# A planner's rule that holds VectorE and ScalarE for urgent operations, an earlier landing time, and 18 idle products instead of 22

## The chip, the cores and the metric

The kernel runs on 1 core of one Trainium2 chip. The metric is the device time of one execution in microseconds (us). The median of three runs of the kernel before is 561.59 us, the lowest 561.55, the highest 562.51.

The names of the engines: TensorE is PE in the rows (PEld is its weight load), VectorE is DVE, ScalarE is ACT, GpSimd is POOL and SyncE is SP, which issues most transfers.

## The reference

Two layers of a decoder trunk over 256 positions of width 1024. Each layer makes RMSNorm of x, one wide input projection (5452 + 3072 columns), and from its parts three token mixers: a gated DeltaNet (short convolution, chunked delta rule with a triangular solve, 4 heads), a pooling mixer, and sparse attention in which an indexer picks 64 keys per query. Their outputs are gated, projected, merged and projected again.

```python
def hybrid_layer(x, ...):
    h = rms_norm(x, norm_g)
    proj = jnp.einsum('btd,de->bte', h, w_in)
    (qa, ka, va, za, ba, aa, ub, zb, qc, kc, vc, zc, iq, ik, iw, gates) = split_columns(proj)
    ya = deltanet_branch(qa, ka, va, za, ba, aa, conv_w, a_log, dt_bias, dn_onorm)
    yb = pooling_branch(ub, zb, pool_w, pool_scale)
    yc = sparse_attention_branch(qc, kc, vc, zc, iq, ik, iw, q_norm, k_norm, ...)
    branches = jnp.stack([ya, yb, yc], axis=2)
    projected = jnp.einsum('btnc,ncd->btnd', branches, w_branch)
    gate = jax.nn.sigmoid(gates.reshape(b, t, N_BRANCH, D_MODEL) + gate_b)
    return x + jnp.einsum('btd,de->bte', jnp.sum(gate * projected, axis=2), w_out)
```

In DeltaNet the decay is the exponential of differences of a cumulative sum g, and the solve is of a unit lower triangular matrix per chunk of 64. In the attention, scores outside the chosen keys are put to minus infinity before the softmax.

## The kernel before

Activations and weights are float32; TensorE multiplies them as three products of a shorter type: a weight tile comes by DMA into `raw` (5 buffers of 128 x 1024), a CAST makes its high part `wh` (6 buffers, ScalarE, or VectorE where the planner chooses it), VectorE subtracts and makes the low part `wl` (5 buffers). In the same way the normed input is `hh` and `hl`. TensorE then does wh with hh, wh with hl, and wl with hh, into one of four PSUM banks `pj`; other products and transposes go to four banks `mx`.

The order of the work is not written by hand. The code lists every operation with what it reads and writes (`Plan.add`), and `Plan.lay_out` sorts the list onto the five engines with a model of each engine's time (`cost`), of the transfers' landing times, and of the delay from one engine to another (`LAG`, and `MARGIN` of 400 ns for TensorE). On each engine the operation that is ready and has the least rank comes next; the rank is the order in the program for TensorE, and elsewhere the latest start `late`, which `deadlines` works out backwards from the end of the last pass. Six passes (`PASSES`) are made and the shortest kept. Each engine then runs its instructions in that order and waits for others by semaphores. A buffer or PSUM bank goes to the next user when its last reader is done in the plan.

`pick` chooses the next operation of one engine at the time that the engine is free. `soon` holds operations that become ready later, `now` those that are ready. `EARLY` is a time in ns that is added to a transfer's expected landing if it is issued before `CALM` (10000 ns in the plan), `DELAY` the same for later ones. The `NWARM` products at the start multiply a zeroed `wh` tile by itself and their result is not used.

Names that come up below: `gh` and `gl` are the two parts of the log decay of the heads, `sgr` a constant matrix of ones that sums them up, and the `wl` tiles written from `cs` and `gh` are the decay's factors (they take two of the `wl` buffers); `score` and `top` are the scores and the eight highest values of one round of the top-k; `big` holds the attention's logits, `sm4` their sums and `ri` their reciprocals, `nb` the negative maximum; `uc` are the diagonal 32 x 32 blocks of the triangular matrices, `xi` and `xb` belong to the recurrence that inverts them (31 steps on VectorE), `cv` is the scale of the transposed v, `u` are working tiles; `rs` is the norm's factor.

Of the kernel before, what the change touches and what calls it, by code (L numbers as in the profile page):

```python
# [42 lines left out]
LATE, X1, CRIT, BACK = 200, 138, ((-600, 0), (-600, -500)), 300  # L43

KOUT = 4
NWARM = 22

SWITCH = 103.0

# [1 line left out]

MARGIN = 400.0

EARLY, DELAY, CALM = 900.0, 900.0, 10000.0

SLACK = 300.0

LATER = 21000.0

# [207 lines left out]
class Plan:  # L267
# [168 lines left out]
    def lay_out(self):  # L436
# [12 lines left out]
        soon = {e: [] for e in engines}  # L449
        now = {e: [] for e in engines}  # L450
# [26 lines left out]
        def uses(o, e):  # L477
            return o.other[4] if o.other and e == o.other[0] else o.port

        def held(o, e):  # L480
            return o.other[2] if o.other and e == o.other[0] else o.cost

        def fill(o):
            return o.args[0].shape[0] * o.args[1].shape[0] / 16384.0

        def clear(o, e, t):


            if e in shared and uses(o, e):
                t = max(t, shared["POOL" if e == "DVE" else "DVE"])  # L490
            if e != "PE":
                for z in o.tiles:
                    if z.tag.psum and z.reader != e:
                        t = max(t, z.until)
            return t

        def live(q):
            return self.ops[q[-2]].start is None and self.ops[q[-2]].turn == q[-1]

        def pick(e):  # L500

            while soon[e] and not live(soon[e][0]):
                heapq.heappop(soon[e])
            while now[e] and not live(now[e][0]):
                heapq.heappop(now[e])
            t = free[e]
            while soon[e] and soon[e][0][0] <= t:
                q = heapq.heappop(soon[e])
                if live(q):
                    heapq.heappush(now[e], q[1:])  # L510
            if not now[e]:
                while soon[e] and not live(soon[e][0]):
                    heapq.heappop(soon[e])
                if not soon[e]:
                    return None
                q = soon[e][0][1:]
                return clear(self.ops[q[1]], e, soon[e][0][0]), e, q
            if e == "PE" and not small and t < whole + REST and fill(self.ops[now[e][0][1]]) < 0.6:
                for q in heapq.nsmallest(40, now[e]):
                    if live(q) and fill(self.ops[q[1]]) > 0.9:  # L520
                        return t, e, q
            first = now[e][0]
            at = clear(self.ops[first[1]], e, t)
            if at > t:
                for q in heapq.nsmallest(12, now[e]):
                    o = self.ops[q[1]]
                    if live(q) and clear(o, e, t) <= t and held(o, e) <= at - t + SLACK:
                        return t, e, q
            return at, e, first

        for o in self.ops:
# [3 lines left out]
        while len(order) < len(self.ops):  # L535
            best = None
            for e in engines:
                c = pick(e)
                if c and (best is None or c[:2] < best[:2]):
                    best = c  # L540
# [4 lines left out]
            at, e, q = best  # L545
            o = self.ops[q[1]]
# [85 lines left out]
def trunk(ctx: ExitStack, tc: tile.TileContext, x, xt, gain, w_in, gate_b, pool_w, w_branch, w_out, cst0, cst1, cst2, cst3,  # L632
# [44 lines left out]
    def bank(tag):  # L677
        return plan.tile(tags[tag], [128, 512])
# [66 lines left out]
    wp = bank("mx")  # L745
    for i in range(NWARM):
        PE.matmul(wp[:, :256], warm[:, :128], warm, start=True, stop=True)
# [758 lines left out]
```

## Time and profile before

| | |
|---|---|
| median of 3 runs | 561.59 us (561.55 to 562.51) |
| profiled execution | 561.43 us, span 559.50 us |
| TensorE busy | 553.1 us (99%), 3434 instructions |
| TensorE weight load busy | 487.0 us (87%) |
| VectorE busy | 499.1 us (89%), 1111 instructions |
| ScalarE busy | 325.7 us (58%), 658 instructions |
| GpSimd busy | 22.0 us (4%) |
| DMA | 99.79 MB, mean 178 GB/s |

Busy is the sum of an engine's durations. Matmuls are pipelined and their ends are modelled, so the busy time of TensorE overlaps with the next product's; the starts are the better measure. On a timeline, a row is a run of like instructions; its first number is the start of the first one, and the number in front of the engine's name is the time that they take. What stands in square brackets is the idle time in front of the row and who ended it.

### The profile page before, as it was taken

What the parts mean: (1) busy time and instruction counts of PE and PEld (TensorE: products, weight loads), DVE (VectorE), ACT (ScalarE), POOL (GpSimd) and SP (SyncE); (2) the same over time, 40 slices, a digit from 0 to 9 for tenths busy, and PEclk for the clock granted to TensorE, in tenths of its full rate; (3) what the DMA queues carried; (4) which work ended last, traced back from release to release, by engine and by line L of the source; (5) the groups of instructions that cost most, each with busy time, mean ns of one, the idle gap of its engine ahead of it and who ended that gap; (6) DMA issues with size and microseconds to landing.
All of it is one profiled execution on the core that took longest, in us unless ns stands there. A gap on an engine that the chain in (4) does not pass through costs nothing.

```text
span 559.5 us, 9552 instructions
## 1 busy us (share of the span) xinstructions
PE 553.1 (99%) x3434; PEld 487.0 (87%) x3434; DVE 499.1 (89%) x1111; ACT 325.7 (58%) x658; POOL 22.0 (4%) x31
## 2 busy tenths in 40 slices
PE   9999999999999999999999999999999999999997
PEld 8978999999888887888879789999998888788886
DVE  6999999999999999687689999799999999967672
ACT  8795786668543526463466675866584444455530
POOL 0200000000000000000010010000000000000000
PEclk9999999999999999999999999999999999999999
DMA  8845484383866656334447346346356667445402
GB/s 321 304 153 202 156 274 149 107 274 83 279 206 205 208 190 223 136 131 151 148 140 229 115 153 219 114 149 214 124 196 214 209 188 230 120 152 201 156 32 76
DMA packets 29855, 99.79 MB, mean 178 GB/s; under 512 B 3312, under 2 KB 4080, under 8 KB 29808
## 3 DMA queue, kind: packets, MB, share of 16 engines
q1 hardware_dynamic: 29232, 98.22, 53.4%
q0 software_dynamic: 288, 0.64, 0.4%
q8 instruction: 27, 0.44, 0.3%
q10 hardware_dynamic: 288, 0.33, 0.2%
q14 instruction: 20, 0.16, 0.1%
HBM read 98.12 MB, written 1.05 MB: 177 GB/s over the span
## 4 chain that ended last, share of the span: by engine, by line
PE 86%; DVE 9%; ACT 3%; issue 1%; POOL 0%; DVEq 0%; POOLq 0%
PE pj L627 69%; PE mx L627 17%; DVE wl L627 3%; DVE u L627 2%; DVE score L627 2%; ACT wh L627 1%; ACT u L627 1%; DVE top L627 1%; DVE hl L627 1%; ACT wl L627 1%; ACT big L627 0%; DVE big L627 0%; POOL r4k L627 0%; ACT uc L627 0%; ACT kiT L627 0%
## 5 line engine op out<-in xcount | busy, mean ns | idle before, releaser
L627 ACT CAST wh<-raw 128x1024 fp32r<-128x1024 f32 (+2 forms) x169 | 174.8, 1040 | 136.1 <-PE pj L627 104.5
L627 DVE TENSOR_TENSOR wl<-raw,wh 128x1024 fp32r<-128x1024 f32 (+2 forms) x176 | 209.1, 1201 | 14.4 <-PE pj L627 4.9
L627 PE MATMUL pj<-wh,hh 128*128 128x512 f32 (+1 forms) x352 | 103.0, 389 | 0.0
L627 PE MATMUL pj<-wh,hl 128*128 128x512 f32 (+1 forms) x352 | 101.2, 387 | 1.1 <-DVE hl L627 1.1
L627 PE MATMUL pj<-wl,hh 128*128 128x512 f32 (+1 forms) x352 | 101.4, 387 | 0.0
L627 PEld LDWEIGHTS pj<-wh,hl 128*128 128x128 f32 x352 | 65.2, 188 | 13.8 <-DVE hl L627 1.5
L627 PEld LDWEIGHTS pj<-wh,hh 128*128 128x128 f32 x352 | 64.6, 188 | 12.6 <-ACT hh L627 0.4
L627 PEld LDWEIGHTS pj<-wl,hh 128*128 128x128 f32 x352 | 65.0, 188 | 12.1
L627 PE MATMUL pj<-hh,wh 128*128 128x256 f32 x384 | 56.3, 285 | 0.0
L627 PE MATMUL pj<-hh,wl 128*128 128x256 f32 x384 | 55.3, 284 | 0.0
L627 PE MATMUL pj<-hl,wh 128*128 128x256 f32 x384 | 55.2, 284 | 0.0
L627 PE MATMUL pj<-wh,y 128*128 128x512 f32 (+1 forms) x208 | 51.5, 383 | 0.0
L627 PEld LDWEIGHTS pj<-hh,wh 128*128 128x128 f32 x384 | 50.4, 191 | 0.3
L627 PEld LDWEIGHTS pj<-hh,wl 128*128 128x128 f32 x384 | 50.1, 192 | 0.1
L627 PEld LDWEIGHTS pj<-hl,wh 128*128 128x128 f32 x384 | 50.0, 192 | 0.0
L627 PEld LDWEIGHTS pj<-wh,y 128*128 128x128 f32 x208 | 38.5, 188 | 7.5
L627 PE MATMUL mx<-wh,y 128*128 128x512 f32 (+1 forms) x128 | 38.4, 380 | 0.0
L627 PEld LDWEIGHTS mx<-u,u 128*128 128x128 f32 (+2 forms) x336 | 28.7, 164 | 3.0 <-issue 1.8
L627 PE MATMUL mx<-u,u 128*128 128x128 f32 (+2 forms) x336 | 30.4, 250 | 0.0
L627 DVE SCALAR_TENSOR_TENSOR u<-pj,cs,u 128x255 f32<-128x255 f32 (+2 forms) x72 | 29.1, 472 | 0.5 <-ACT u L627 0.5
L627 PE MATMUL pj<-wl,y 128*128 128x512 f32 (+1 forms) x104 | 28.5, 382 | 0.0
L627 PEld LDWEIGHTS mx<-wh,y 128*128 128x128 f32 x128 | 23.3, 188 | 4.4 <-DVE y L627 0.2
(203 smaller groups left out, 679.9 us busy)
## 6 DMA issues: line engine op xcount, KB each, us to landing
raw<-in_w_in_dram SPq DMA_DIRECT2D x124, 512.0 KB, 4.3
raw<-in_w_branch_dram SPq DMA_DIRECT2D x24, 512.0 KB, 4.4
raw<-in_w_out_dram SPq DMA_DIRECT2D x16, 512.0 KB, 3.5
tg<-in_gate_b_dram SPq DMA_DIRECT2D x12, 256.0 KB, 4.8
raw<-in_w_in_dram SPq DMA_DIRECT2D x4, 498.0 KB, 6.2
raw<-in_xt_dram SPq DMA_DIRECT2D x4, 256.0 KB, 4.3
raw<-in_xt_dram SPq DMA_DIRECT2D x2, 512.0 KB, 6.3
x_sb<-in_x_dram SPq DMA_DIRECT2D x2, 512.0 KB, 3.6
```

Of the source, the lines that this page charges most:

```text
L627: getattr(self.real[o.eng], o.call)(*[put(a) for a in o.args], **{k: put(v) for k, v in o.kw.items()})
```

## The change

Three numbers change (18 idle products, `EARLY` of 300, and a new `HASTE` of 0), and `pick` gets a rule for VectorE and ScalarE. The rule looks at the operation `o` that would be taken next and at the time `stop` at which it would end. If one of the four operations that become ready first, `z`, is ready before `stop` and its `late` is before `stop`, `o` is not taken. In its place comes another ready operation that ends before `z` is ready, or else `z` itself, for which the engine stands still until it is ready. An exception is an `o` that would itself be late if `z` went first.

```diff
-NWARM = 22
+NWARM = 18
...
-EARLY, DELAY, CALM = 900.0, 900.0, 10000.0
+EARLY, DELAY, CALM = 300.0, 900.0, 10000.0
...
+HASTE = 0.0
...
+            if e in ("DVE", "ACT"):
+                o = self.ops[first[1]]
+                stop = at + held(o, e)
+                for q in heapq.nsmallest(4, soon[e]):
+                    z = self.ops[q[2]]
+                    if live(q) and z.late is not None and q[0] < stop and z.late < stop - HASTE:
+
+                        if o.late is None or o.late < q[0] + held(z, e):
+                            break
+                        for p in heapq.nsmallest(12, now[e]):
+                            s = self.ops[p[1]]
+                            if live(p) and clear(s, e, t) + held(s, e) <= q[0] + HASTE:
+                                return clear(s, e, t), e, p
+                        return clear(z, e, q[0]), e, q[1:]
             return at, e, first
```

The orders that come of it differ in many places. TensorE has 3210 products instead of 3214 (the four idle ones). VectorE makes ten of the 128 x 1024 CASTs of `wh` instead of six, ScalarE four fewer.

VectorE at the boundary of the layers, before (numbers behind a name are buffers, `mx3_122` is a bank):

```order
L627 TENSOR_SCALAR big3_114<-big3_114,rs0_200 128x512
L627 TENSOR_TENSOR wl4_78<-raw3_66,wh2_70 128x1024
L627 TENSOR_TENSOR wl3_77<-raw4_67,wh1_69 128x1024
L627 TENSOR_TENSOR wl0_74<-raw0_63,wh4_72 128x1024
L627 TENSOR_TENSOR hl0_80<-mx1_120,hh0_79 128x4x128
L627 TENSOR_TENSOR x_sb0_123<-x_sb0_123,mx0_119 128x512
L627 TENSOR_TENSOR hl0_80<-mx3_122,hh0_79 128x4x128
```

and now:

```order
L643 TENSOR_SCALAR big3_114<-big3_114,rs0_200 128x512
L643 TENSOR_TENSOR wl3_77<-raw3_66,wh2_70 128x1024
L643 TENSOR_TENSOR wl4_78<-raw4_67,wh1_69 128x1024
L643 TENSOR_TENSOR hl0_80<-mx1_120,hh0_79 128x4x128
L643 TENSOR_TENSOR x_sb0_123<-x_sb0_123,mx0_119 128x512
L643 TENSOR_TENSOR hl0_80<-mx2_121,hh0_79 128x4x128
```

The third `wl` has moved from in front of both `hl` to behind them.

ScalarE at the decay of layer 0, before:

```order
L627 ACTIVATE wl2_76<-cs0_124,gl0_170 128x128 x4
L627 ACTIVATE eg0_171<-mx1_120 128x16
L627 ACTIVATE wl3_77<-cs0_124,gh0_169 128x128 x4
L627 ACTIVATE u4_100<-mx0_119 128x512
L627 ACTIVATE big3_114,sm40_176<-big3_114,nb0_174,r4q0_156 128x128 x4
L627 ACTIVATE wl3_77<-cs0_124,gl0_170 128x128 x2
L627 ACTIVATE big3_114<-big3_114,ri0_178 128x128
L627 ACTIVATE wl3_77<-cs0_124,gl0_170 128x128 x2
L627 ACTIVATE big3_114<-big3_114,ri0_178 128x128 x3
```

and now:

```order
L643 ACTIVATE wl2_76<-cs0_124,gl0_170 128x128 x4
L643 ACTIVATE eg0_171<-mx2_121 128x16
L643 ACTIVATE wl3_77<-cs0_124,gh0_169 128x128 x4
L643 ACTIVATE wl3_77<-cs0_124,gl0_170 128x128 x4
L643 ACTIVATE u10_106<-mx3_122 128x512
L643 ACTIVATE u11_107<-mx2_121 128x512
L643 CAST wh5_73<-raw0_63 128x1024
L643 ACTIVATE f0_94<-pj0_115 128x512
L643 CAST wh0_68<-raw1_64 128x1024
L643 ACTIVATE big3_114,sm40_176<-big3_114,nb0_174,r4q0_156 128x128 x4
```

The second decay tile is now finished without a break, and the exponentials of the softmax (`big`, `sm4`) come behind two copies, two CASTs and a gate. On VectorE nine instructions of the top-k (four MATCH_REPLACE and three MAX of 128 columns, one of each of 256) have moved from in front of `gh` to behind it.

ScalarE at the scaling of v of layer 0, before:

```order
L627 CAST y2_83<-big3_114 128x256
L627 COPY uc0_184<-u10_106 32x128 x3
L627 ACTIVATE f1_95<-pj0_115 128x512
L627 COPY uc0_184<-u10_106 32x128
L627 ACTIVATE u13_109<-mx0_119,cv0_183 128x128 x4
L627 ACTIVATE u11_107<-mx3_122,cv0_183 128x128 x4
```

and now:

```order
L643 CAST y2_83<-big3_114 128x256
L643 ACTIVATE f1_95<-pj0_115 128x512
L643 COPY uc0_184<-u11_107 32x128
L643 ACTIVATE u7_103<-mx0_119,cv0_183 128x128 x4
L643 COPY uc0_184<-u11_107 32x128
L643 ACTIVATE u13_109<-mx2_121,cv0_183 128x128 x4
L643 COPY uc0_184<-u11_107 32x128 x2
```

Of the four COPYs one stands in front of the scalings from `mx0` now, and three behind them.

## Rows read from the trace of the kernel before

**Rows 1.** Page, part 1: busy time, share of the span, instructions
```profile
PE 553.1 (99%) x3434; PEld 487.0 (87%) x3434; DVE 499.1 (89%) x1111; ACT 325.7 (58%) x658; POOL 22.0 (4%) x31
```

**Rows 2.** Timeline 81 to 84.4 us, TensorE: start, us, engine, line, op
```profile
81.38 1.12 PE L627 MATMUL pj<-hh,wh 128*128 128x256 f32 x8
82.34 0.52 PE L627 MATMUL pj<-hl,wh 128*128 128x256 f32 x3
82.90 0.44 PE L627 MATMUL mx<-cs,big 128*128 128x128 f32 x2
```

**Rows 3.** Timeline 276 to 291 us, TensorE, then VectorE (layer boundary)
```profile
281.04 0.39 PE L627 MATMUL mx<-wl,y 128*128 128x512 f32 x1
281.27 0.63 PE L627 MATMUL pj<-wh,hh 128*128 128x512 f32 x2
282.99 0.73 PE L627 MATMUL pj<-wh,hl 128*128 128x512 f32 x2 [1.09 <-DVE hl L627]
...
278.85 3.49 DVE L627 TENSOR_TENSOR wl<-raw,wh 128x1024 fp32r<-128x1024 f32 x3
282.25 0.69 DVE L627 TENSOR_TENSOR hl<-mx,hh 128x512 fp32r<-128x512 f32 x1
```

**Rows 4.** Timeline 52 to 72 us, ScalarE, then TensorE (decay products, layer 0)
```profile
58.20 1.28 ACT L627 ACTIVATE wl<-cs,gh 128x128 fp32r<-128x128 f32 x4 [3.05 <-DVE gh L627]
...
61.39 0.39 PE L627 MATMUL pj<-hl,wh 128*128 128x256 f32 x2
61.95 0.50 PE L627 MATMUL mx<-wl,sgr 128*128 128x512 f32 x1 [0.17 <-ACT wl L627]
...
65.15 0.64 PE L627 MATMUL pj<-hh,wl 128*128 128x256 f32 x4
65.81 0.50 PE L627 MATMUL mx<-wl,sgr 128*128 128x512 f32 x1
```

**Rows 5.** Groups of VectorE by form: count | busy, mean ns | idle before
```profile
L627 DVE MATCH_REPLACE8 score<-top,score 128x256 f32<-128x256 f32 x16 | 6.6, 410 | 0.0
...
L627 DVE MATCH_REPLACE8 score<-top,score 128x128 f32<-128x128 f32 x16 | 4.4, 276 | 0.0
L627 DVE CAST wh<-raw 128x1024 fp32r<-128x1024 f32 x6 | 4.1, 684 | 0.0
```

**Rows 6.** Timeline 132 to 139 us, TensorE, then ScalarE (transposes of q, layer 0)
```profile
135.31 0.60 PE L627 MATMUL mx<-y,wl 128*128 128x256 f32 x3
136.40 0.66 PE L627 MATMUL mx<-cs,u 128*128 128x128 f32 x4 [0.49 <-ACT u L627]
...
133.33 0.91 ACT L627 COPY uc<-u 32x128 f32<-32x128 f32 x3 [0.63 <-DVE u L627]
...
135.20 2.18 ACT L627 ACTIVATE u<-mx,cv 128x128 f32<-128x128 f32 x8
```

**Rows 7.** Timeline 346 to 351 us, TensorE, then ScalarE (softmax, layer 1)
```profile
349.03 0.64 PE L627 MATMUL pj<-hh,wl 128*128 128x256 f32 x4
349.81 0.33 PE L627 MATMUL mx<-cs,big 128*128 128x128 f32 x1
...
348.34 1.04 ACT L627 CAST wh<-raw 128x1024 fp32r<-128x1024 f32 x1
```

**Rows 8.** Timeline 0 to 14 us, TensorE and its weight loads (start)
```profile
1.09 5.06 PE L627 MATMUL mx<-wh 128*128 128x256 f32 x22 [1.09 <-POOL wh L627]
...
8.08 0.19 PEld L627 LDWEIGHTS pj<-wh,hh 128*128 128x128 f32 x1 [0.22 <-ACT big L627]
```

**Rows 9.** Timeline 66 to 72 us, TensorE (first softmax, layer 0)
```profile
70.47 0.60 PE L627 MATMUL mx<-cs,big 128*128 128x128 f32 x4
```

**Rows 10.** Windows: us, busy (x) of PE PEld DVE ACT POOL, clock, DMA, GB/s
```profile
284.00:480.00 196.00, 195.86 (x1229) 176.03 (x1228) 187.79 (x455) 118.60 (x250) 7.98 (x8) 1.00 0.56 179
```

**Rows 11.** Timeline 478 to 482 us, VectorE, then TensorE (recurrence, layer 1)
```profile
479.42 0.91 DVE L627 STREAM_TRANSPOSE u<-xi 128x256 f32<-128x256 f32 x2
...
480.71 0.45 PE L627 MATMUL mx<-u,u 32*32 32x32 f32 x32
```

## The prediction

> **What bounds the kernel now.** I read the totals of the page first [rows 1]. TensorE is busy for 553.1 of the 559.50 us span, VectorE for 499.1, ScalarE for 325.7. A busy TensorE is not yet one at its pace, so I took the pace from the timeline: eight products of 256 columns start at 81.38 and the next group starts at 82.34 [rows 2], which is 0.96/8 = 0.120 us each, and a product of 512 columns takes 0.23 (281.04 to 281.27) [rows 3]. Where rows follow each other at these paces nothing is left to win. What can be won is a place where a row starts later than the row before it, plus count times pace, allows. I went through the whole of TensorE's timeline for such places, and six remain that the change touches. The engines that TensorE waits for there are VectorE and ScalarE; what they do in front of the awaited instruction decides.
>
> The profiled execution took 561.43 us, 1.93 us outside its span. It is 0.16 us under the median of 561.59, so I sum against 561.43 and add 0.16 at the end.
>
> **The change part by part: the waits that go.** A row's end by pace is its start plus count times pace; the gap to the next row is the price.
>
> Layer boundary [rows 3]. Two products with hh start at 281.27, so TensorE is free at 281.27 + 2 x 0.23 = 281.73. The product with hl starts at 282.99: a wait of 1.26 us. VectorE does three wl in a row from 278.85 and hl only at 282.25, so one wl takes (282.25 - 278.85)/3 = 1.13 us. The products of 281.27 read hh already, so hl cannot be kept by hh any later than that. In the changed order one of the three wl stands behind both hl. Then hl starts at 278.85 + 2 x 1.13 = 281.11, 1.13 earlier, or at 281.27 if hh comes no sooner (0.98 earlier). I take 1.1 us of the 1.26. The wl that moved is first wanted two weight tiles later, so it has a few us of room.
>
> Decay products of layer 0 [rows 4]. ScalarE stands for 3.05 us until VectorE delivers gh at 58.20; the wl tiles that it then makes are late for TensorE: 61.39 + 2 x 0.120 = 61.63 against 61.95, and 65.15 + 4 x 0.120 = 65.63 against 65.81. That is 0.32 + 0.18 = 0.50 us. In the changed order nine top-k instructions (seven of 128 columns, two of 256) come behind gh. By the groups' means [rows 5] these are about 7 x 0.276 + 2 x 0.410 = 2.8 us busy, and about 0.08 us of each lies beside its neighbour, so gh is some 2.1 us earlier. ScalarE then makes both decay tiles without the exponentials of the softmax in between. Both waits are shorter than 2.1, so I take 0.5.
>
> Softmax transposes at 82.90 [rows 2]: 82.34 + 3 x 0.120 = 82.70, a wait of 0.20. The softmax comes no later than before while TensorE's other work in between is the same, so I take the 0.2; the bounds are 0 and 0.2.
>
> Transposes of q in layer 0 [rows 6]: 135.31 + 3 x 0.120 = 135.67 against 136.40, 0.73 us. The bank is freed by four of ScalarE's eight scalings, which start at 135.20 behind four COPYs uc. Three COPYs take 0.91 us. After the change one COPY stands ahead of the first four scalings and three behind, so these may be up to 0.9 earlier, less if the Tanh that now comes first is itself awaited. Bounds 0 and 0.73; I take 0.5, nearer to the upper end because the three COPYs alone cover the whole wait. The COPYs that come later feed the recurrence, which by the order begins ten and more long instructions of VectorE later, so nobody waits for them.
>
> Softmax transposes of layer 1 [rows 7]: 349.03 + 4 x 0.120 = 349.51 against 349.81, 0.30 us. ScalarE's CAST of 1.04 us at 348.34 stands in front of the scaling that is awaited; after the change this CAST is done by VectorE ahead of the reciprocal at 0.684 us [rows 5], and the wl that delayed the reciprocal follows it. TensorE's transposes are ordered a little earlier too, so I take 0.2 of 0 to 0.3.
>
> Start [rows 8]. Four of 22 idle products at 5.06/22 = 0.23 us are 0.9 us. This is hardly won, because the first real operands set the pace: with 22 idle products ahead the weight load at 8.08 still waited 0.22 us for another engine, and the first transfers land no sooner. I take 0.1; the ends are 0 and 0.9, and the row of the wait lies nearer to 0. The smaller EARLY only changes what the plan believes of the first transfers; the transfers are the same, but for an order of SyncE's first constants and one weight transfer that it issues three places later, and a small operation of GpSimd that comes behind two constant loads; what TensorE waits for at the start is in the bound of 0 to 0.9 already.
>
> The gains are 1.1 + 0.5 + 0.2 + 0.5 + 0.2 + 0.1 = 2.6 us; with every wait gone wholly 1.26 + 0.50 + 0.20 + 0.73 + 0.30 + 0.22 (the load's wait at the start) = 3.21.
>
> **The waits that come.** The first softmax of layer 0 pays for the earlier gh: its exponentials stood among the decay tiles on ScalarE and now stand behind two copies, two CASTs and a Tanh; VectorE gives nb0 about 5.8 us later by its order (five wl between the last top-k steps and nb0, at 1.13 each). The transposes that need it stood at 70.47 [rows 9] and are ordered at about the same place. I count the chain as ending between 70 and 72, so the wait is 0 to 1.0 us; I take 0.3.
>
> VectorE's own work: four CASTs wh go from ScalarE to VectorE, 4 x 0.684 = 2.7 us [rows 5], and some copies. In layer 1 between hl and the end of the recurrence it has about 3.3 us more by count, of which 1.1 is the wl that moved past hl, so 2.2 are new. The cover is VectorE's idle time there: from 284 to 480 it is busy 187.8 of 196 us [rows 10], 8.2 idle. The transposes that end the recurrence are done at 479.42 + 0.91 = 480.33 and TensorE takes them at 480.71 [rows 11], so about 0.3 us of slack is left. Not all of the idle time lies where it can be used; I take 0.5 us of new wait at the recurrences' ends, with bounds 0 and 2.
>
> Net: 2.6 - 0.3 - 0.5 = 1.8 us. 561.43 - 1.8 = 559.6, and with 0.16 the median is 559.8.
>
> **A rule weighed against the trace.** The granted clock of the profile reads 1.00 from the start, the upper level of 2.4 GHz, yet the idle products take 0.23 us each [rows 8] and those of the same size later 0.120 [rows 2]; the real products that follow run at the later pace. The Trainium skill, "TensorE: Matmul & The Clock Gate", section "Part 1: The HAM clock gate", says that the default state is throttled and activity releases it, at an instant that differs between runs; by that rule the idle products are what lifts the clock, and fewer of them could lift it later. By the rows the real products would then fill the gap at the slow pace, as in the fourth rival; by the rule as by the rows nothing is lost if TensorE goes on without a pause.
>
> **The rivals.** The recurrence takes it back. VectorE is nearly full in both recurrences. If the transposes that end them come no earlier than before, TensorE waits there for what it gained ahead. For: the small slack of 0.3 [rows 11]. Against: idle time of 8.2 us [rows 10]. If only layer 0 loses its gain and layer 1 keeps 1.1 + 0.2 = 1.3, 561.6 - 1.3 = 560.3; if both lose most, 560.9 to 561.6. Chance 0.25.
>
> Slower: VectorE's extra work in layer 1 isn't absorbed. Place: the wait at 480.71. If layer 0's gain is lost at its recurrence, and hl starts 1.1 earlier but 3.3 more work follows, the transposes end at 480.33 - 1.1 + 3.3 = 482.5 less what is absorbed; TensorE took them at 480.71. With nothing absorbed that is 1.8 later: 561.4 + 1.8 + 0.16 = 563.4. It decides where less than 0.7 us of the 3.3 is absorbed, 1.8 less the 1.1 that a measurement can tell. For: TensorE waits for VectorE there at 0.3 us of slack. Against: the idle time. Chance 0.09.
>
> The clock comes later. If fewer idle products leave a pause before the first real one and the upper pace begins some 0.9 us later, about four real products cost 0.23 more each, 0.9 us: 560.7. For: 0.9 us of products are gone. Against: the pause lies after products that already ran for 4 us. Chance 0.05.
>
> The change does all that it says and no wait comes: all 3.21 us, 558.4. Chance 0.10.
>
> The likeliest case is the sum, 558.9 to 560.6 by its bounds, 0.51.
>
> **How the numbers follow.** A measurement can tell 0.2%, 1.1 us, from no change here: faster is under 560.5, slower over 562.7. Faster: 0.51 x 0.95 of the likeliest, 0.10 of the full gain, and 0.07 of the recurrence case where only layer 0 loses, together 0.65. Slower: the slower rival, 0.09. Same: the rest, 0.26. The range 558.3 to 562.0 reaches from the full gain to the recurrence case and leaves out mostly the slower rival; the likeliest one's own is 558.9 to 560.6.
>
> **What would show it.** After the change the row of hl products behind the pair at the layer boundary should start within 0.2 us of its pace, gh should come about 2 us earlier against TensorE, and the rows at the transposes of q and the two softmax transposes should have no gap over 0.2. At the two recurrences' ends a gap of up to 0.5. The start should end its idle products 0.9 earlier and reach the first 512-column pace as before. I am wrong if gaps over 0.5 appear at the ends of the recurrences or at layer 0's first softmax, or if the boundary wait stays over 0.5.

## The result, and the profile after

The changed kernel takes 559.19 us (median of 6 runs, 559.05 to 559.35) against 562.06 us (6 runs, 561.55 to 563.27) for the kernel before. The ratio is 0.9949, with an interval of 0.9939 to 0.9959: about 2.9 us faster. The forecast was 559.8 us, 1.8 us faster than the profile of before. The two profiled executions differ by less than the medians, 559.5 to 557.4 us of span: the runs of before spread by 1.7 us, and its profiled execution (561.43 us) was shorter than all six. The terms of the forecast are compared with these 2.1 us.

The totals of the page after, to be read against [rows 1]:

```profile
PE 552.3 (99%) x3430; PEld 485.7 (87%) x3430; DVE 502.3 (90%) x1115; ACT 323.0 (58%) x654; POOL 24.4 (4%) x31
```

TensorE's products are the same but for the four idle ones, so what counts are the waits. At the layer boundary, TensorE and then VectorE (start us, us, engine, line, op):

```profile
280.89 0.63 PE L643 MATMUL pj<-wh,hh 128*128 128x512 f32 x2
281.48 0.73 PE L643 MATMUL pj<-wh,hl 128*128 128x512 f32 x2
...
278.47 2.35 DVE L643 TENSOR_TENSOR wl<-raw,wh 128x1024 fp32r<-128x1024 f32 x2
280.74 0.68 DVE L643 TENSOR_TENSOR hl<-mx,hh 128x512 fp32r<-128x512 f32 x1
...
284.47 1.22 DVE L643 TENSOR_TENSOR wl<-raw,wh 128x1024 fp32r<-128x1024 f32 x1
285.61 0.48 DVE L643 TENSOR_SCALAR big<-big,rs 128x512 f32<-128x512 f32 x1
```

This answers to [rows 3]: from 280.89 the pace gives 281.35, and the hl products start at 281.48, 0.13 late where it was 1.26. The third wl now starts at 284.47, after both hl and after the norm of the second half, and the scaling of `big` follows it at 285.61.

The decay products and the first softmax of layer 0, ScalarE and then TensorE:

```profile
56.22 1.28 ACT L643 ACTIVATE wl<-cs,gh 128x128 fp32r<-128x128 f32 x4 [3.23 <-DVE gh L643]
...
60.72 0.76 PE L643 MATMUL pj<-hh,wl 128*128 128x256 f32 x5
61.31 0.40 PE L643 MATMUL mx<-wl,sgr 128*128 128x512 f32 x1
...
70.69 0.52 PE L643 MATMUL pj<-hh,wh 128*128 128x256 f32 x3
71.41 0.33 PE L643 MATMUL mx<-cs,big 128*128 128x128 f32 x1 [0.20 <-ACT big L643]
```

ScalarE starts on gh at 56.22 instead of 58.20 [rows 4], and makes both decay tiles without a break, the last four operations from 59.81. The wl,sgr row of 61.31 stands at its pace (60.72 + 5 x 0.12 = 61.32). The first softmax is what is late now: 70.69 + 3 x 0.12 = 71.05 against 71.41, a new wait of 0.36 us.

The transposes of q, TensorE, then ScalarE, GpSimd and VectorE:

```profile
134.94 0.48 PE L643 MATMUL mx<-y,wl 128*128 128x256 f32 x2
135.68 0.66 PE L643 MATMUL mx<-cs,u 128*128 128x128 f32 x4 [0.26 <-ACT u L643]
...
134.32 0.30 ACT L643 COPY uc<-u 32x128 f32<-32x128 f32 x1 [0.21 <-DVE u L643]
134.53 1.10 ACT L643 ACTIVATE u<-mx,cv 128x128 f32<-128x128 f32 x4
...
130.20 1.72 POOL L643 TENSOR_TENSOR rk<-ssk,mhalf 128x4 f32<-128x4 f32 x1 [6.96 <-DVE ssk L643]
...
131.95 0.16 DVE L643 TENSOR_TENSOR cc<-beta,rk 128x4 f32<-128x4 f32 x1 [0.56 <-POOL rk L643]
...
133.17 1.12 DVE L643 SCALAR_TENSOR_TENSOR u<-mx,cn,u 128x128 f32<-128x128 f32 x4
...
134.54 0.15 DVE L643 SCALAR_TENSOR_TENSOR cv<-ssk,rk 128x4 f32<-128x4 f32 x1
```

and VectorE before:

```profile
132.17 1.12 DVE L627 SCALAR_TENSOR_TENSOR u<-mx,cn,u 128x128 f32<-128x128 f32 x4
```

Here the wait is still there: 134.94 + 2 x 0.12 = 135.18 against 135.68, 0.5 us (0.42 by the start of the last product of the row, 135.14). The four scalings that free the bank start at 134.53, right behind the one COPY that is left in front of them, and this COPY waits for VectorE's u. That u ends at 133.17 + 1.12 = 134.29, where before it was 132.17 + 1.12 = 133.29: VectorE stood 0.56 us for GpSimd's factor rk, which took 1.72 us. The scalings do not wait for the cv of 134.54. It starts after them and belongs to the second half of the positions; in the kernel the first four scalings read the cv of the first half. The second transposes, at 137.16, are 0.16 late (136.54 + 2 x 0.23 = 137.00), since the other four scalings come behind the first.

The softmax of layer 1 [rows 7], the start [rows 8] and the end of the recurrence of layer 1 [rows 11]:

```profile
346.61 0.89 PE L643 MATMUL pj<-hl,wh 128*128 128x256 f32 x6
347.33 0.27 PE L643 MATMUL mx<-cs,big 128*128 128x128 f32 x1
...
5.11 0.80 PE L643 MATMUL pj<-wh,hh 128*128 128x512 f32 x1
5.71 0.45 PE L643 MATMUL pj<-wh,hl 128*128 128x512 f32 x1
...
6.64 0.50 PE L643 MATMUL pj<-wh,hh 128*128 128x512 f32 x1 [0.26 <-ACT wh L643]
...
477.54 0.91 DVE L643 STREAM_TRANSPOSE u<-xi 128x256 f32<-128x256 f32 x2
...
478.54 0.39 PE L643 MATMUL pj<-wl,hh 128*128 128x512 f32 x1
478.85 0.45 PE L643 MATMUL mx<-u,u 32*32 32x32 f32 x32
```

The transposes of 347.33 follow 346.61 + 6 x 0.12 at once. At the start the real products begin 0.85 us sooner, but the first takes 0.60 us and after the third TensorE waits for wh until 6.64. At the recurrence's end TensorE takes the transposes 0.08 us after its pace (478.54 + 0.23 = 478.77 against 478.85).

Put together, by the starts of the same row in both traces (a row of hh,wh products at 14 us: 14.11 before, 14.25 after; of hl,wh at 55: 54.74 and 55.08; the hh pair at the boundary: 281.27 and 280.89; wl,hh behind it: 283.56 and 282.05; the end of the span):

| part | forecast, us | measured, us |
|---|---|---|
| start, up to 55 us | -0.1 | +0.34 |
| decay products -0.5, first softmax +0.3, 82.90 -0.2 | -0.4 | -0.72 |
| transposes of q | -0.5 | 0.0 |
| recurrences' ends | +0.5 | 0.0 |
| layer boundary | -1.1 | -1.13 |
| layer 1 | -0.2 | -0.6 |
| sum | -1.8 | -2.1 |

### The profile page after: what moved, and what is told of

Same layout as the page of the kernel before. It is cut to its first block, busy times and chain, and to the rows that moved or that the text cites. A ratio compares the mean times of both kernels' runs of the same rounds, so it can differ in the third digit from the quotient of the medians.

```text
span 557.4 us, 9530 instructions
## 1 busy us (share of the span) xinstructions
PE 552.3 (99%) x3430; PEld 485.7 (87%) x3430; DVE 502.3 (90%) x1115; ACT 323.0 (58%) x654; POOL 24.4 (4%) x31
## 4 chain that ended last, share of the span: by engine, by line
PE 89%; DVE 7%; issue 1%; ACT 1%; DMA 1%; POOL 0%; DVEq 0%; POOLq 0%
PE pj L643 72%; PE mx L643 17%; DVE u L643 2%; DVE wl L643 1%; DVE score L643 1%; DVE big L643 1%; DVE top L643 1%; DMA x_sb<-in_xt_dram 1%; ACT big L643 1%; POOL rk L643 0%; ACT wh L643 0%; DVE hl L643 0%; DVE x_sb L643 0%; ACT u L643 0%; ACT hh L643 0%
## 5 line engine op out<-in xcount | busy, mean ns | idle before, releaser
L643 ACT CAST wh<-raw 128x1024 fp32r<-128x1024 f32 (+2 forms) x165 | 170.7, 1040 | 133.0 <-PE pj L643 104.7
```

The source lines that it names most:

```text
L643: getattr(self.real[o.eng], o.call)(*[put(a) for a in o.args], **{k: put(v) for k, v in o.kw.items()})
```

## The experiments

Times are medians. The runs of before that stand beside them have medians of 561.67, 562.05 and 561.68 us in the three sets, so a ratio says more than a difference over sets. Two kinds of edit were used. One changes the planner, which then makes another plan everywhere. The other keeps a plan word for word and moves single operations in it after it is made:

```diff
-        for o in self.plan():
+        order = self.plan()
+        at = {o.n: o for o in order}
+        for n, side, m in [...]:
+            order.remove(at[n])
+            order.insert(order.index(at[m]) + side, at[n])
+        for o in order:
             getattr(self.real[o.eng], o.call)(...)
```

### The planner's edits one by one

The changed kernel without the rule (norule), and the kernel before with the rule alone (ruleonly), both as edits of the changed kernel:

```diff
-            if e in ("DVE", "ACT"):
+            if False:
```

> The changed kernel without the new rule (18 idle products and the landing time of 300 stay). Theory 1 (the rule brings the gain): the time of before, within 0.5 us. Theory 2 (any other plan loses the bad order at the layer boundary, since here too one subtraction fewer stands in front of hl): 1.1 to 2.0 us faster than before.

```diff
-NWARM = 18
+NWARM = 22
...
-EARLY, DELAY, CALM = 300.0, 900.0, 10000.0
+EARLY, DELAY, CALM = 900.0, 900.0, 10000.0
```

> The kernel before with the new rule alone (22 idle products, landing time 900). By its order the boundary has two subtractions in front of hl too, and gh has twelve to sixteen top-k instructions in front of it, fewer than before. Theory (boundary and layer-0 waits carry the gain, whichever edit brings the order): 1.1 to 2.4 us faster than before. Rival (rule and landing time are needed together): less than 0.7 us faster.

Measured: 560.97 us without the rule (ratio 0.9979, 0.997 to 0.9988, runs from 559.3 to 561.5), and 561.75 us with the rule alone (ratio 0.9992, 0.9984 to 1.0001). Theory 1 fails for norule, since part of the gain comes without the rule, and theory 2 (1.1 to 2.0 us) fits the 1.2 us of its ratio. The rule alone brings nothing that can be told: its rival holds. Yet in both traces the waits at the boundary and at the layer-1 softmax are gone, as in the changed kernel. Each pays for them in layer 0. TensorE, then GpSimd, without the rule:

```profile
22.98 0.46 PE L643 MATMUL pj<-wh,hh 128*128 128x332 f32 x2
24.53 0.33 PE L643 MATMUL mx<-cs,u 128*128 128x128 f32 x1 [1.08 <-ACT u L643]
...
20.89 3.15 POOL L643 TENSOR_TENSOR r4k<-se,mhalf 128x4 f32<-128x4 f32 x1 [0.21 <-DVE se L643]
```

TensorE and then ScalarE with the rule alone:

```profile
136.09 0.48 PE L643 MATMUL mx<-y,wl 128*128 128x256 f32 x2
138.03 0.66 PE L643 MATMUL mx<-cs,u 128*128 128x128 f32 x4 [1.46 <-ACT u L643]
...
134.53 0.61 ACT L643 COPY uc<-u 32x128 f32<-32x128 f32 x2 [1.98 <-DVE u L643]
...
136.84 2.17 ACT L643 ACTIVATE u<-mx,cv 128x128 f32<-128x128 f32 x8
```

Without the rule 22.98 + 2 x 0.15 gives 23.28, and the transposes start at 24.53: 1.25 us late, since GpSimd's r4k takes 3.15 us. A further 0.35 is lost at 28.8 and 0.73 at 63.2. With the rule alone the transposes of q are 1.7 us late (138.03 against 136.09 + 0.24), as the scalings of v begin only at 136.84, behind COPYs that wait 1.98 us for VectorE's u, and at 62.27 the decay products are 0.8 late. So the boundary's gain belongs to neither edit; each of the three plans has it. What the three edits together bring is a plan that has it and does not pay in layer 0. By the orders that the planner makes, without a run of them, the rule acts on VectorE only: restricted to ScalarE it gives the plan without the rule, restricted to VectorE the plan of the changed kernel, row for row. The landing time with 22 idle products was not run, so norule's share is that of the two numbers together; the number of idle products alone leaves the plan as it was (b18 below).

### The idle products

The plan of before with 18 (b18), and the plan of the changed kernel with the idle product issued four times more (a22, its second edit, cut):

```diff
-NWARM = 22
+NWARM = 18
...
+            for _ in range(5 if o.n in (20,) else 1):
```

> The order of before with 18 idle products instead of 22 and nothing else. Theory (the first operands set the pace): the same time within 0.3 us. Rival 1 (the idle products were in the way): 0.8 us faster. Rival 2 (TensorE's pace rises later): 0.5 to 1 us slower, and products of 512 columns at 0.43 us each for a while after the first.

> The order of the changed kernel, with 22 idle products at the start instead of 18 (the plan is still the one made for 18). Theory (the first operands set the pace): the same as the changed kernel within 0.3 us. Rival (fewer idle products cost 0.3 us at the start, as the changed kernel's trace has TensorE 0.34 us behind at 40 us): 0.3 us faster than the changed kernel.

Measured: 561.38 us (ratio 0.9994, 0.9985 to 1.0003) and 559.21 us (0.9954, 0.9942 to 0.9966) against 559.19 with 18. The theory holds: four idle products more or less are nothing. But the reason is not only that operands are late. TensorE of b18:

```profile
5.25 0.79 PE L627 MATMUL pj<-wh,hh 128*128 128x512 f32 x1
5.84 0.63 PE L627 MATMUL pj<-wh,hl 128*128 128x512 f32 x1
6.27 0.60 PE L627 MATMUL pj<-wl,hh 128*128 128x512 f32 x1
6.70 0.41 PE L627 MATMUL pj<-wh,hh 128*128 128x512 f32 x1
6.94 0.40 PE L627 MATMUL pj<-wh,hl 128*128 128x512 f32 x1
```

The products from 5.25 to 6.70 start 0.43 to 0.59 us apart and from 6.70 on 0.24; with 22 the first real product starts at 5.96, the next 0.31 later, and from there the starts are 0.23 apart. So in this run the products that replace idle ones go at about half the pace.

The traced run of a22 also shows how far one place moves from run to run: its order in layer 1 is that of the changed kernel, but at the softmax of layer 1 it loses 0.7 us more (its profiled execution took 559.94 us).

### The layer boundary by itself

The plan of before with the third wl moved: once behind both hl only (b_wl2), once behind the norm of the second half too (b_wl3). The transfer that reuses the wl's source buffer moves with it. A first version without that (b_wl) let the transfer overwrite the buffer before the subtraction read it, so that the wl was that of another weight tile; the subtraction waited 4.18 us for that transfer, TensorE stood for 5.5 us up to 291.53, and the time was 567.48 us.

```diff
+        for n, side, m in [(2586, 1, 2554), (2814, 1, 2586)]:   # b_wl2: 2586 wl, 2554 hl, 2814 transfer
+        for n, side, m in [(2586, 1, 2559), (2814, 1, 2586)]:   # b_wl3: 2559 the last product of big
```

> The order of before with the third wl subtraction of the layer boundary behind both hl, and the transfer that reuses its raw buffer behind it. Theory (the boundary wait is that one subtraction): 1.1 us faster than before, the wait of 1.26 falls to about 0.13. Rival (the time is given back in layer 1, by the later transfer or at the recurrence's end): less than 0.4 us faster.

> The order of before with the third wl subtraction of the layer boundary (and the transfer that reuses its buffer) behind the whole chain of the second half: hl, hl, f, se and the two products of big, where the changed kernel has it. Theory 1 (in b_wl2 the subtraction stood in front of that chain, so its end stayed where it was and TensorE waited 1.21 us there): both waits go, 1.0 to 1.2 us faster than before. Theory 2 (the time is given back later in layer 1 by VectorE): under 0.4 us faster.

Measured: 561.74 us (ratio 1.0001, 0.9992 to 1.001) and 561.45 us (0.9998, 0.9988 to 1.0007). Neither gain that was expected, 1.1 and 1.0 to 1.2 us, came. The wait is gone at its place in both (b_wl3: hl products at 282.08, 0.13 behind the pace from 281.49) and stands a few us later. TensorE and VectorE of b_wl2:

```profile
286.32 0.62 PE L632 MATMUL pj<-wh,hh 128*128 128x512 f32 x2
287.99 0.66 PE L632 MATMUL mx<-cs,big 128*128 128x128 f32 x4 [1.05 <-ACT big L632]
...
283.62 1.22 DVE L632 TENSOR_TENSOR wl<-raw,wh 128x1024 fp32r<-128x1024 f32 x1
284.75 0.69 DVE L632 SCALAR_TENSOR_TENSOR f<-x_sb 128x512 f32<-128x512 f32 x1
```

and of b_wl3:

```profile
286.79 0.47 PE L632 MATMUL pj<-wh,hl 128*128 128x512 f32 x1
287.85 0.66 PE L632 MATMUL mx<-cs,big 128*128 128x128 f32 x4 [0.59 <-DVE big L632]
...
285.08 2.32 DVE L632 TENSOR_TENSOR wl<-raw,wh 128x1024 fp32r<-128x1024 f32 x2
287.32 0.48 DVE L632 TENSOR_SCALAR big<-big,rs 128x512 f32<-128x512 f32 x1
```

In b_wl2 the wl at 283.62 stands in front of f, so the norm of the second half ends no sooner than before, and the transposes of `big` wait 1.21 us (286.32 + 0.46 against 287.99). In b_wl3 the norm is sooner, but now two wl (2.32 us) stand in front of the scaling of `big` at 287.32, and 0.83 is lost; by the starts in its trace 0.3 of the 1.13 us stays won. The plan of the changed kernel has one wl between norm and scaling, and the next one behind the scaling; there the whole 1.13 stays won. That this second move is what keeps it is read from the orders; the plan of before with both moves was not run. The traced run of b_wl2 (562.95 us, 1.2 over its median) lost another 1.0 us at the softmax of layer 1, which the median does not show.

### VectorE's room in the recurrence

The changed kernel with two wl subtractions of the recurrence of layer 1 issued twice (a_rec2):

```diff
-            getattr(self.real[o.eng], o.call)(...)
+            for _ in range(2 if o.n in (4253, 4477) else 1):
+                getattr(self.real[o.eng], o.call)(...)
```

> The changed kernel with two wl subtractions of layer 1's recurrence (at about 414 and 452 us) done twice: 2 x 1.13 = 2.3 us more for VectorE. Theory of the forecast's slower rival (VectorE has about 0.4 us of slack at the recurrence's end and no idle time before it there): TensorE waits about 1.9 us at 479 and the time rises by 1.6 to 2.0 us. Rival (VectorE's idle time of the recurrence, 2.7 us, absorbs it): less than 0.5 us.

Measured: 560.95 us (ratio 0.9981, 0.9971 to 0.999), 1.8 us over the changed kernel. TensorE:

```profile
479.09 0.39 PE L644 MATMUL pj<-wl,hh 128*128 128x512 f32 x1
481.00 0.45 PE L644 MATMUL mx<-u,u 32*32 32x32 f32 x32 [1.52 <-DVE u L644]
...
480.50 0.91 DVE L644 STREAM_TRANSPOSE u<-xi 128x256 f32<-128x256 f32 x2
```

479.09 + 0.23 = 479.32 against 481.00: 1.68 us. Of 2 x 1.13 = 2.26 us more work about 0.6 is covered, so work that VectorE gets late in the recurrence does come through to TensorE, as the slower rival had it. The row of VectorE's two transposes ends at 480.50 + 0.91 = 481.41, after TensorE's start: TensorE waits for the first of the two alone. The rival itself did not happen: in the changed kernel the transposes start 1.9 us sooner (477.54 against 479.42 in [rows 11]), as TensorE does (2.1), so the new work of VectorE in layer 1 was absorbed ahead of them. From the first hl of the layer to these transposes VectorE is busy 189.0 of 197.2 us before and 191.6 of 196.8 us after. Its idle time falls most around the softmax, from 2.8 us (342 to 360 before) to 0.7 (340.5 to 357.9 after), and by 1.0 in the first 18 us.

### The place of gh

The changed kernel with nine top-k instructions in front of gh again (a_gh):

```diff
+        for n, side, m in [(n, 0, 515) for n in (278, 304, 279, 305, 280, 306, 281, 307, 282)]:   # 515 gh
```

> The changed kernel with the nine top-k instructions in front of gh again. Theory (gh 2.5 us later brings back TensorE's waits for the decay tiles, 0.7 us in the trace of before, partly spared since ScalarE makes both tiles in one go): 0.4 to 0.9 us slower than the changed kernel. Rival (these waits were ScalarE's order, not gh's): the same within 0.2 us.

Measured: 562.40 us, ratio 1.0008 (1.0 to 1.0017), 3.2 us over the changed kernel. TensorE, and its windows (us, busy of PE, PEld, DVE, ACT, POOL, granted clock, DMA, GB/s):

```profile
56.03 0.39 PE L648 MATMUL mx<-u,u 128*128 128x128 f32 x2
58.84 0.27 PE L648 MATMUL mx<-gh,upr 128*128 128x8 f32 x1 [2.43 <-DVE gh L648]
...
58.00:61.00 3.00, 2.16 (x13) 2.16 (x14) 2.97 (x13) 2.18 (x8) 0.00 (x0) 0.76 0.00 0
61.00:64.00 3.00, 3.00 (x18) 2.86 (x18) 2.92 (x5) 3.00 (x11) 0.00 (x0) 0.68 0.66 214
```

Both theories fall. The changed plan has moved TensorE's products with gh forward too, so without gh TensorE stands for 2.6 us, and then runs below its clock for some us: 0.76 and 0.68 granted, and 1.00 again from 64 to 70. Product by product against the changed kernel, TensorE is 2.6 us late behind the pause and 4.2 us late from 63 us on, so the clock costs 1.6; waits further on take 1.0 of it back. The runs show the same price: in nine of the eleven the granted clock of the whole run is 0.997 and the time 562.2 to 563.3 us, in the other two it is 1.000 and the time 560.80 and 560.97 us. gh's place and TensorE's order belong together, and about half of the 3.2 us is the clock.

### Filling the waits that are left

a_q moves cv on VectorE and four scalings on ScalarE forward; a_best adds later transposes on TensorE:

```diff
+        for n, side, m in [(1457, 1, 1455), (1565, 0, 1462), (1566, 0, 1462), (1567, 0, 1462), (1568, 0, 1462)]:   # a_q
+        ... + [(676, 1, 765), (677, 1, 767), (678, 1, 768), (679, 1, 769), (1585, 1, 1721), (1586, 1, 1585), ...]   # a_best
```

> The changed kernel with cv moved on VectorE from behind the four cn operations to in front of them, and the four scalings of v that free the bank moved on ScalarE in front of the COPY uc. Theory (TensorE's wait of 0.42 us at the transposes of q is for cv, 1 us late): cv about 2 us earlier, the wait gone, 0.4 us faster than the changed kernel. Rival (the transposes of v or the gate in front on ScalarE are next): 0 to 0.2 us.

> The changed kernel with the edits of a_q, the four transposes of the first softmax two or three products later on TensorE, and the last transposes of q two products later. Theory (the waits of 0.36 and 0.31 us are filled with products that are ready): 0.6 to 0.9 us faster than the changed kernel. Rival (the wait moves to the next place that needs these transposes, or VectorE's recurrence takes it back at 217 us): 0 to 0.3 us.

Measured: 559.20 us for a_q (ratio 0.9951, 0.9939 to 0.9963) and 558.71 us for a_best (0.995, 0.9938 to 0.9963). In a_q the 0.42 us are gone, but 0.31 stand at the second four transposes, which the second four scalings set; the rival is right. The run does not show that the wait was for cv: the edit also takes the four scalings out from behind the COPY, and by the rows above that is what they stood behind. In a_best these waits are filled, and the first softmax's transposes follow without a gap (70.88 + 6 x 0.12 = 71.60). Its span is 557.0 us against 557.4 and its median half a microsecond lower, but by the ratios, 0.995 against 0.9949, nothing is left of that. The 0.6 to 0.9 us that were expected are not shown.

### GpSimd's factor

a_port moves three VectorE operations with both operands in SBUF away from beside rk:

```diff
+        for n, side, m in [(1249, 1, 1456), (1253, 1, 1249), (1252, 1, 1253), (1447, 1, 1440), (1254, 1, 1252)]:
```

> The changed kernel with three VectorE operations whose operands lie in SBUF (two y, one big) moved away from beside GpSimd's factor rk at 130 us; two additions that read PSUM stand there instead. Theory (GpSimd's operation is held up by VectorE's operations on two SBUF operands beside it, 1.72 us against 1.01 alone): rk takes 1.0 to 1.1 us. Rival (its length has nothing to do with VectorE): 1.7 again. The time stays within 0.4 us of the changed kernel.

Measured: rk 1.01 us, and 559.68 us (ratio 0.9968, 0.9957 to 0.9979). That is 0.5 us over the changed kernel by the medians and 1.1 by the ratios, more than the 0.4 expected. For rk it looks like the theory, but a_best, whose neighbours of rk are those of the changed kernel, shows 1.04 in its profile, and b_wl2, whose order there is that of before (1.04), shows 1.71. GpSimd's rows of a_best and b_wl2:

```profile
130.38 1.04 POOL L648 TENSOR_TENSOR rk<-ssk,mhalf 128x4 f32<-128x4 f32 x1 [6.96 <-DVE ssk L648]
```
```profile
129.93 1.71 POOL L632 TENSOR_TENSOR rk<-ssk,mhalf 128x4 f32<-128x4 f32 x1 [7.80 <-DVE ssk L632]
```

So one order gives either length from run to run, and the run is inconclusive. What lengthens these operations stays open.

## Why the prediction was right, point by point

The sum was 0.3 us short of what the profiles show, and 1.1 short of the medians. That it came so close is luck in part: single terms were wrong by up to 0.5 us, and their errors cancel.

- Layer boundary: right in size, 1.1 against 1.13. The reason given was not complete. That the third wl goes behind both hl wins nothing alone (b_wl2), and behind the norm 0.3 at most (b_wl3); the transposes of the second half's `big`, five us behind, take the rest. I said of the moved wl only that it has room, and did not follow the chain of the second half that it shares VectorE with. The changed plan happens to clear that as well, which the forecast did not count on.
- Decay products and first softmax: right in mechanism. gh came 2.0 us earlier (2.1 forecast), its waits went, and the first softmax cost 0.36 (0.3 forecast, 0 to 1.0). The decay term was too small: counted product by product, TensorE goes from 0.34 late at 55 us to 0.66 early at 68, so it won 1.0 where 0.5 was forecast. Among it is a wait of 0.28 before that I had not counted (59.26 + 3 x 0.12 = 59.62 against 59.90):

```profile
59.26 0.60 PE L627 MATMUL pj<-hh,wh 128*128 128x256 f32 x3
59.90 0.47 PE L627 MATMUL mx<-wl,sgr 128*128 128x512 f32 x1
```

- Softmax transposes at 82.90: 0.2 forecast, about 0.1 won.
- Transposes of q: wrong, 0.5 forecast, 0 measured. The step took the 0.91 us of the three COPYs in front of the scalings for the price. They did move, but the one COPY that is left in front still waits for VectorE's u, as [rows 6] has it (0.63 <-DVE u), and u came 1.0 us later than before. About half of that is VectorE's wait for GpSimd's rk, 1.72 us instead of 1.04. So the first scalings start only 0.7 us sooner, 0.3 against TensorE, and what this wins at the first transposes stands as a new wait at the second.
- Softmax of layer 1: mis-sized. 0.2 forecast and up to 0.3 by its wait, about 0.6 measured, all of it between 346 and 356 us. The transposes stand earlier in TensorE's order and nothing takes it back. The traces of norule and ruleonly have the same 0.6; a22's shows that a run can lose as much here.
- Start: wrong sign by 0.4 us. That the start wins nothing is right (b18, a22). The loss is not the idle products': with 22 in the changed plan the time is the same. Of the 0.34 us 0.14 are there at 14 us; the rest comes at small waits between 18 and 40 us, where the forecast had counted no change. The 0.22 us of the weight load at 8.08, a term of the full gain, cost TensorE next to nothing: the products at 7.89 and 8.13 start 0.24 apart.
- Recurrences: 0.5 forecast, none measured. The slack was read too small: I took the end of both transposes (480.33), but TensorE needs only the first (a_rec2, where 0.6 us was covered). The new work, 2.2 us by count and 2.6 by the busy times, was absorbed by idle time ahead of the recurrence's end, most of it around the softmax of layer 1.
- The clock rival: real products in place of idle ones do run at the slow pace (b18), but the time is the same with 18 or 22, as the idle ones ran at that pace too.

The rule named in the changed code was not the cause by itself: alone it brings at most 0.9 us and probably nothing, and the other two edits alone 1.2 us by the ratio (0.7 to 1.7). The gain is that of a plan, not of a rule. Why the planner's three edits make just this plan was not followed.

## What to carry to other kernels

Behind an operation moved out of an urgent one's way, follow every chain that shares its engine for the next few microseconds, not only the operation's own reader: a wait of 1.26 us fell to 0.14, and one of 1.21 us came five us later. With a planner, judge an edit by the waits of the plan that comes of it, place by place; the same rule with the old landing time and 22 idle products gave nothing that could be told. And where a whole plan is moved to rely on an early value, putting that value back can cost more than it won (3.2 us, half of it by the clock, where the whole stretch had won 0.7).

## What the runs showed of the hardware

A pause of TensorE of 2.6 us (a_gh) was followed by stretches with a granted clock of 0.76 and 0.68, that is partly at 1.2 instead of 2.4 GHz, in the traced run and by the time in eight more, but not in two of the eleven. A pause of 5.5 us (b_wl) was followed by 0.56 (290 to 296 us) and 0.87 (296 to 302). One of 1.7 us (a_rec2) was not followed by any: 1.00 from 478 to 484 us, and the products behind 481.00 keep the pace of 0.23. The Trainium skill, "TensorE: Matmul & The Clock Gate", section "Part 1: The HAM clock gate", says that the throttled state is the default and that activity releases it; the trace agrees for the longer pauses: in a_gh 0.68 from 61 to 64 us, after TensorE had taken up work at 58.84, and 1.00 from 64 us on. During the idle products at the start the rows give a granted clock of 1.00 though the products go at half the pace (0.23 us for 256 columns against 0.120 later).

GpSimd's rk on 128 x 4 elements took 1.01 to 1.98 us (ruleonly) and r4k up to 3.69 us (norule), the former with the same neighbours 1.04 or 1.71. The Trainium skill, "SBUF — State Buffer", section "SBUF: two separate sides", says that VectorE's operations with two SBUF inputs and GpSimd's operations that read SBUF take a shared port for a whole instruction each, and the other waits. a_port (1.01 us without such neighbours) agrees; a_best (1.04 with them) shows no such wait, so no run here shows that the port is the cause. TensorE's waits behind such an operation reached 1.25 us (norule).
